# A decoder layer in float32r: the sixteen means of squares as two float32r passes instead of one float32 matmul

## The chip, the core and the metric

The kernel runs on one core of one Trainium2 chip. The metric is device microseconds (us) of one execution; the times below are of three runs. The profile is of one further execution of the same program.

## The reference

One inference step of a one-layer decoder, for a prompt of 256 tokens and a sample batch of 8 x 8 tokens (320 columns together), width 2048:

```
z = rmsnorm(x, g_mix) @ w_in                      # 2048 -> 3584
b, c, hc, q, k, v, qx = split(z)                  # conv gates, 8 q heads, 2 kv heads, 4 cross heads
q, k, qx = rmsnorm(q), rmsnorm(k), rmsnorm(qx)    # per head of 128
y_conv = b * short_conv(c * hc)
y_swa  = sink_attention(q, k, v, window 128, relative bias)
y_x    = cross_attention(qx, memory keys, memory values)
x = x + concat(y_conv, y_swa, y_x) @ w_out
x = x + square(relu(rmsnorm(x, g_mlp) @ w_up)) @ w_down
rmsnorm(x, g) = x * rsqrt(mean(x * x) + 1e-6) * g
```

## The kernel before

**Layout and the large products.** Activations lie transposed: features on the 128 partitions, the 320 tokens along the free axis. A weight piece (128 x 2 x 512) is loaded into `raw` (four buffers), split by ScalarE into its rounded part `wh` (float32r) and by VectorE into the rest `wl`, and each product is three float32r matmuls of 128x320, `wh` by S0h, `wh` by S0l, `wl` by S0h (lines 462 to 464), where S0h and S0l (later S1h and S1l) are the activations split in the same way. These are the rows `mm<-S0h,wh` and so on. A group is one block of 512 output columns: 192 such matmuls into four PSUM banks `mm`. The groups go in the order: cross q, k and v, memory k, memory v (these two with 512 columns), q0, q1, C, H, B, four groups of w_out, then w_up and w_down in four rounds. There are four `mm` banks, so the first matmul into a bank of the next group waits until the bank was read out ("evacuated").

**The side jobs.** All small work (norms, attention, bias) is written as Python generators, the jobs (`Side`, line 206). After each unit of 12 matmuls `boundary()` runs evacuations that are due, and then lets each active job issue its next piece (`side.step()`). A job asks for a buffer (`need`) or waits in a Python model of the engines' clocks (`Pace`, line 93; `after`, line 272) before it issues. So numbers in `Pace.cost` and the count of `yield`s set where a job's instructions stand in each engine's queue. On the chip each engine then takes its queue in that order, and waits at the head of it until the operand is there.

**The means.** A mean of squares over the 128 partitions is one float32 matmul with a matrix of constants, so that the mean stands on every partition: `ones_d` (1/2048) in `mean_rsqrt` (line 517; used for `rb`, the input norm's factor, and once for the MLP norm), `ones_h` (1/128) in `start_head` (line 580; once for each of 4 cross heads, 2 k heads and 8 q heads). Sixteen in all. `newton_terms` (line 353) follows on ScalarE: Ln, Exp, Square.

**Two places where the program holds the matmuls back.** The evacuations of the first group multiply by `rb`, so the second group's first matmul cannot be issued before rb's job has finished (`if waiting: side.until(["rb"])`). And the evacuation of the first bank of group C needs a buffer that the prompt's cross attention gives back:

```
def c_evac(m, ps):
    if m == 0:
        side.until(["convpre"])
```

`side.until` issues side jobs step by step, and no large matmul, until the named job is done. "convpre" (line 1035) waits for "cp", `cross_prompt_all` (line 770), which works off the four cross heads one after another: scores into a bank, maximum, exponential, reciprocal, scaling, four transposes, copy, product with the values.

`z` tiles come from ten slots (`zs`, line 269); a head holds z and y and later a.

Of the kernel before, what the change touches and what calls it, by code (L numbers as in the profile page):

```python
# [9 lines left out]
F32 = mybir.dt.float32  # L10
F32R = mybir.dt.float32r
AF = mybir.ActivationFunctionType
ALU = mybir.AluOpType
AX = mybir.AxisListType

P = 128
# [6 lines left out]
T = TP + TS  # L23
# [224 lines left out]
def trunk_step(ctx: ExitStack, tc: tile.TileContext, I, O):  # L248
# [4 lines left out]
    pe, act, dve = (Paced(pace, n, e) for n, e in (("pe", nc.tensor), ("act", nc.scalar), ("dve", nc.vector)))  # L253
    pool, sp = Paced(pace, "pool", nc.gpsimd), Paced(pace, "dma", nc.sync)

    const = ctx.enter_context(tc.tile_pool(name="const", bufs=1))
# [12 lines left out]
    zs = Slots(zp, "z", 10)  # L269
    lx = Slots(lxp, "lx", 4)  # L270

    def after(*tiles):
        while not pace.ready(tiles):
            yield 1

    def bank():
        return ax.need([P, 512])

    def zt(cols=336):
        return zs.need([P, 336])  # L280

    def sm(n=8):
        return smp.tile([P, 8], F32, name="sm", tag="sm")
# [21 lines left out]
    ones_h = const.tile([P, P], F32, name="ones_h")  # L305
    dve.memset(ones_h, 1.0 / 128)
    ones_d = const.tile([P, P], F32, name="ones_d")
    dve.memset(ones_d, 1.0 / D)
    eps = const.tile([P, 1], F32, name="eps")
    dve.memset(eps, EPS)  # L310
    col["n_q"], col["n_k"], col["n_x"] = 63, 64, 65
# [29 lines left out]
    def small_rsqrt(out, ss, n, width):  # L341
        v, y, t = sm()[:, 0:n], sm()[:, 0:n], sm()[:, 0:n]
        dve.tensor_scalar(out=v, in0=ss, scalar1=1.0 / width, scalar2=EPS, op0=ALU.mult, op1=ALU.add)
        yield from after(v)
        act.activation(out=y, in_=v, func=AF.Ln)
        act.activation(out=y, in_=y, func=AF.Exp, scale=-0.5)
        act.activation(out=t, in_=y, func=AF.Square)
        yield from after(t)
        dve.tensor_tensor(out=t, in0=v, in1=t, op=ALU.mult)
        dve.tensor_scalar(out=t, in0=t, scalar1=-0.5, scalar2=1.5, op0=ALU.mult, op1=ALU.add)  # L350
        dve.tensor_tensor(out=out, in0=y, in1=t, op=ALU.mult)

    def newton_terms(y, a, mean):
        act.activation(out=y, in_=mean, func=AF.Ln, bias=eps)
        act.activation(out=y, in_=y, func=AF.Exp, scale=-0.5)
        act.activation(out=a, in_=y, func=AF.Square)
        yield from after(a)
        dve.scalar_tensor_tensor(out=a, in0=mean, scalar=EPS, in1=a, op0=ALU.add, op1=ALU.mult)
# [158 lines left out]
    def mean_rsqrt(out, sq):  # L517

        yield from after(sq)
        bk = yield from bank()  # L520
        pe.matmul(out=bk[:, 0:T], lhsT=ones_d, rhs=sq, start=True, stop=True)
        yield 1
        y = yield from zt()
        yield from newton_terms(y[:, 0:T], out, bk[:, 0:T])
        ax.put(bk)
        dve.tensor_scalar(out=y[:, 0:T], in0=y[:, 0:T], scalar1=-0.5, scalar2=None, op0=ALU.mult)
        dve.scalar_tensor_tensor(out=out, in0=out, scalar=-3.0, in1=y[:, 0:T], op0=ALU.add, op1=ALU.mult)
        zs.put(y)

    def rb_job():  # L530
        for b in range(4):
            act.activation(out=xblk[b], in_=xblk[b], func=AF.Square)
            if b % 2:
                yield 1
                dve.tensor_tensor(out=xblk[b - 1], in0=xblk[b - 1], in1=xblk[b], op=ALU.add)
        yield 1
        s = xblk[0]
        dve.tensor_tensor(out=s, in0=s, in1=xblk[2], op=ALU.add)
        lx.put(xblk[1], xblk[2], xblk[3])
        dve.tensor_tensor(out=s[:, 0:2, :], in0=s[:, 0:2, :], in1=s[:, 2:4, :], op=ALU.add)  # L540
        dve.tensor_tensor(out=s[:, 0, :], in0=s[:, 0, :], in1=s[:, 1, :], op=ALU.add)
        yield from mean_rsqrt(rb, s[:, 0, :])
        lx.put(s)

    def mem_job():
# [27 lines left out]
        ax.put(bk)  # L573
        w2.put(sq)
        yield from small_rsqrt(rm, tot, 2, D)


    turn = [0]

    def start_head(name, ps, gain, dest):  # L580
        z = zs.must([P, 336])
        dve.tensor_tensor(out=z[:, 0:T], in0=ps, in1=rb, op=ALU.mult)

        def gen():
            while side.now < turn[0]:
                yield 1
            turn[0] = side.now + 2
            y = yield from zt()
            yield from after(z)
            act.activation(out=y[:, 0:T], in_=z[:, 0:T], func=AF.Square)  # L590
            yield 1
            yield from after(y)
            bk = yield from bank()
            pe.matmul(out=bk[:, 0:T], lhsT=ones_h, rhs=y[:, 0:T], start=True, stop=True)
            yield 1
            a = yield from zt()
            yield from newton_terms(y[:, 0:T], a[:, 0:T], bk[:, 0:T])
            ax.put(bk)
            dve.scalar_tensor_tensor(out=z[:, 0:T], in0=z[:, 0:T], scalar=gain, in1=y[:, 0:T],
                                     op0=ALU.mult, op1=ALU.mult)  # L600
            zs.put(y)
            dest(lambda out, v: dve.scalar_tensor_tensor(out=out, in0=v(a), scalar=-3.0, in1=v(z),
                                                         op0=ALU.add, op1=ALU.mult))
            zs.put(a, z)

        side.add(name, gen())
# [73 lines left out]
    def mk_job():  # L680
        ss, r = sm(), sm()
        zz = [st.pop("mkz0"), st.pop("mkz1")]
        junk = yield from half()
        for t in range(2):
            for h in range(XH):
                act.activation(out=junk[:, 0:P], in_=zz[t][:, h * P:(h + 1) * P], func=AF.Square,
                               accum_out=ss[:, t * 4 + h:t * 4 + h + 1])
        w2.put(junk)
        yield from after(ss)
        yield from small_rsqrt(r, ss, 8, 128)  # L690
        st["mkT"] = yield from lx.need([P, XH, MEM])
        for t in range(2):
            for h in range(XH):
                s = zz[t][:, h * P:(h + 1) * P]
                dve.scalar_tensor_tensor(out=s, in0=s, scalar=r[:, t * 4 + h:t * 4 + h + 1], in1=gkx,
                                         op0=ALU.mult, op1=ALU.mult)
            pool.dma_start(out=O["p_mk"][0, 0, t * P:(t + 1) * P].rearrange("k h d -> k (h d)"), in_=zz[t])
        for t in range(2):
            yield from after(zz[t])
            bk = yield from bank()  # L700
            for h in range(XH):
                pe.transpose(bk[:, h * P:(h + 1) * P], zz[t][:, h * P:(h + 1) * P], ident)
            yield 1
            act.activation(out=st["mkT"][:, :, t * P:(t + 1) * P], in_=bk.rearrange("p (h k) -> p h k", h=XH),
                           func=AF.Copy)
            ax.put(bk)
            w2.put(zz[t])
# [408 lines left out]
    def out_evac(g):  # L1116
        def f(m, ps):
            k = g * 4 + m
            a = acc[g][:, m, :]
            dve.tensor_tensor(out=a, in0=ps, in1=a, op=ALU.add)  # L1120
            act.activation(out=S0h[:, k, :], in_=a, func=AF.Copy, scale=gcol("g_mlp", k))
            z = st["sqa"] if k == 0 else zs.must([P, 336])
            act.activation(out=z[:, 0:T], in_=a, func=AF.Square)

            def rest():
                dve.scalar_tensor_tensor(out=S0l[:, k, :], in0=a, scalar=gcol("g_mlp", k),
                                         in1=S0h[:, k, :].bitcast(F32), op0=ALU.mult, op1=ALU.subtract)
                if k:
                    dve.tensor_tensor(out=st["sqa"], in0=st["sqa"], in1=z[:, 0:T], op=ALU.add)
                    zs.put(z)  # L1130
                if k == 15:
                    side.add("r2", mean_rsqrt(st["r2b"], st["sqa"]))

            later.append(rest)
        return f
# [65 lines left out]
    bk = ax.must([P, 512])  # L1201
# [74 lines left out]
```

## Time and profile before

| what | value |
|---|---|
| median of three runs | 1342.4 us (1342.21 to 1344.62) |
| the profiled execution's own time | 1342.93 us |
| its span, first to last instruction | 1341.1 us |
| TensorE (PE) busy | 1322.6 us, 99% |
| VectorE (DVE) busy | 655.8 us, 49% |
| ScalarE (ACT) busy | 533.0 us, 40% |
| mean granted TensorE clock | 0.994 |

PE, DVE, ACT, POOL and SP are the five engines; PEld is the weight load, which overlaps PE. Every instruction that passes through the recording helper carries its line, L166, so groups are told apart by their tiles: `mm<-S0h,wh` is a matmul that writes an mm bank. A float32 matmul that isn't a transpose appears as two rows of the trace, a float32r matmul and a transpose as one. A row of the timeline is: start, duration, engine, line, operation, tiles, shape, count, and in brackets the idle time of the engine before it with what ended it. The clock column gives the share of the full TensorE clock that was granted.

### The profile page before, as it was taken

The numbers are of one execution on the slowest core, as the hardware profiler recorded it, in microseconds if no ns is written. First come the engines' busy times: TensorE is split into PE (matmuls) and PEld (weight loads), VectorE is DVE, ScalarE is ACT, GpSimd is POOL, SyncE is SP. The second block draws the span as 40 slices with busy tenths as digits, with TensorE's granted clock in tenths as the row PEclk, the third lists the DMA queues.
The fourth block names the chain that finished last, engine by engine and source line by source line (L and its number), as shares of the span: only waits on it lengthen the run. The fifth ranks groups of instructions, "written<-read, shape, count | busy, mean of one in ns | idle before, by whom it ended". The sixth has DMA issues, their size and how long they took to land.

```text
span 1341.1 us, 21456 instructions
## 1 busy us (share of the span) xinstructions
PE 1322.6 (99%) x8938; PEld 1294.7 (97%) x8938; DVE 655.8 (49%) x974; ACT 533.0 (40%) x771; POOL 15.6 (1%) x32
## 2 busy tenths in 40 slices
PE   8799999999999999999999999999999999999998
PEld 8787999989999999999999999999999999999998
DVE  6575456785455544444344443434444434444342
ACT  7555355433344444323334432233443233444221
POOL 0010000000000000000000000000000000000000
PEclk9899999999999999999999999999999999999999
DMA  8567653436644445444454444444444444445452
GB/s 301 185 203 252 213 182 132 145 111 224 211 157 142 142 148 167 143 157 138 146 161 154 145 139 157 156 152 149 142 141 160 156 156 143 141 150 166 163 175 71
DMA packets 64880, 217.03 MB, mean 162 GB/s; under 512 B 8357, under 2 KB 10125, under 8 KB 64752
## 3 DMA queue, kind: packets, MB, share of 16 engines
q1 hardware_dynamic: 62752, 210.38, 47.4%
q0 software_dynamic: 1744, 5.19, 1.1%
q8 instruction: 70, 1.15, 0.4%
q14 instruction: 26, 0.21, 0.0%
q10 hardware_dynamic: 288, 0.10, 0.0%
HBM read 211.53 MB, written 7.65 MB: 163 GB/s over the span
## 4 chain that ended last, share of the span: by engine, by line
PE 95%; DVE 2%; ACT 1%; DMA 1%; issue 0%; SPq 0%; DVEq 0%; ACTq 0%
PE mm L166 91%; PE ax L166 4%; DVE z L166 1%; DVE wl L166 1%; ACT wh L166 0%; DMA w<-in_cmk 0%; DVE lx L166 0%; DMA raw<-in_w_in 0%; DVE sm L166 0%; ACT lx L166 0%; ACT w L166 0%; DVE w L166 0%; DVE S1l L166 0%; ACT z L166 0%; SPq L166 0%
## 5 line engine op out<-in xcount | busy, mean ns | idle before, releaser
L166 DVE TENSOR_TENSOR wl<-raw,wh 128x1024 fp32r<-128x1024 f32 (+1 forms) x361 | 437.4, 1220 | 557.8 <-ACT wh L166 554.5
L166 ACT ACTIVATE wh<-raw 128x1024 fp32r<-128x1024 f32 (+1 forms) x361 | 375.1, 1053 | 661.7 <-PE mm L166 613.5
L166 PE MATMUL mm<-S0h,wh 128*128 128x320 f32 x1472 | 463.0, 315 | 12.6 <-DVE z L166 9.7
L166 PE MATMUL mm<-S0h,wl 128*128 128x320 f32 x1472 | 456.6, 310 | 0.2 <-DVE wl L166 0.2
L166 PE MATMUL mm<-S0l,wh 128*128 128x320 f32 x1472 | 456.4, 310 | 0.0
L166 PE MATMUL mm<-S1h,wl 128*128 128x320 f32 x1280 | 395.5, 309 | 0.0
L166 PE MATMUL mm<-S1l,wh 128*128 128x320 f32 x1280 | 395.5, 309 | 0.0
L166 PE MATMUL mm<-S1h,wh 128*128 128x320 f32 x1280 | 395.5, 309 | 0.0
L166 PEld LDWEIGHTS mm<-S0h,wh 128*128 128x128 f32 x1472 | 277.9, 189 | 16.5 <-ACT S1h L166 8.2
L166 PEld LDWEIGHTS mm<-S0l,wh 128*128 128x128 f32 x1472 | 278.0, 189 | 0.8
L166 PEld LDWEIGHTS mm<-S0h,wl 128*128 128x128 f32 x1472 | 277.9, 189 | 0.4 <-DVE wl L166 0.4
L166 PEld LDWEIGHTS mm<-S1h,wh 128*128 128x128 f32 x1280 | 240.2, 188 | 0.0
L166 PEld LDWEIGHTS mm<-S1l,wh 128*128 128x128 f32 x1280 | 240.2, 188 | 0.0
L166 PEld LDWEIGHTS mm<-S1h,wl 128*128 128x128 f32 x1280 | 240.2, 188 | 0.0
L166 ACT ACTIVATE z<-z 128x320 f32<-128x320 f32 x108 | 50.0, 468 | 68.6 <-DVE z L166 67.7
L166 DVE TENSOR_TENSOR S1l<-z,S1h 128x320 fp32r<-128x320 f32 x68 | 33.3, 490 | 51.6 <-ACT S1h L166 51.6
L166 DVE TENSOR_TENSOR acc<-mm,acc 128x320 f32<-128x320 f32 x60 | 29.2, 487 | 34.8 <-PE mm L166 34.8
L166 ACT ACTIVATE S1h<-z 128x320 fp32r<-128x320 f32 x68 | 32.1, 472 | 8.7 <-DVE z L166 6.7
L166 DVE SCALAR_TENSOR_TENSOR z<-mm,r2b 128x320 f32<-128x320 f32 x64 | 30.9, 483 | 0.0
L166 PE MATMUL mm<-wh,S1h 128*128 128x512 f32 x64 | 26.2, 410 | 0.0
L166 PE MATMUL mm<-wl,S1h 128*128 128x512 f32 x64 | 25.0, 391 | 0.0
L166 PE MATMUL mm<-wh,S1l 128*128 128x512 f32 x64 | 25.0, 391 | 0.0
(148 smaller groups left out, 418.4 us busy)
## 6 DMA issues: line engine op xcount, KB each, us to landing
raw<-in_w_up SPq DMA_DIRECT2D x128, 512.0 KB, 3.3
raw<-in_w_down SPq DMA_DIRECT2D x128, 512.0 KB, 3.3
raw<-in_w_in SPq DMA_DIRECT2D x56, 512.0 KB, 3.6
raw<-in_w_out SPq DMA_DIRECT2D x32, 512.0 KB, 3.4
raw<-in_w_mem_k SPq DMA_DIRECT2D x8, 512.0 KB, 3.9
w<-in_cmk SPq DMA_DIRECT2D x16, 256.0 KB, 5.6
raw<-in_w_mem_v SPq DMA_DIRECT2D x8, 512.0 KB, 4.1
w<-in_cmv SPq DMA_DIRECT2D x16, 256.0 KB, 4.6
```

The source lines that it names most:

```text
L166: return f(*args, **kw)
```

## The change

Two constant matrices in float32r are added, and a helper that splits the squares into the rounded part (ScalarE copy to float32r) and the rest (VectorE subtraction), and adds up two float32r matmuls into the same bank. Both users of a mean call it.

```
+    mean_h = const.tile([P, P], F32R, name="mean_h")
+    dve.tensor_copy(out=mean_h, in_=ones_h)
+    mean_d = const.tile([P, P], F32R, name="mean_d")
+    dve.tensor_copy(out=mean_d, in_=ones_d)
...
+    def mean_over(bk, y, scale):
+
+        hi = yield from zs.need([P, 336], F32R)
+        lo = yield from zs.need([P, 336], F32R)
+        act.activation(out=hi[:, 0:T], in_=y, func=AF.Copy)
+        dve.tensor_tensor(out=lo[:, 0:T], in0=y, in1=hi[:, 0:T].bitcast(F32), op=ALU.subtract)
+        yield 1
+        yield from after(lo)
+        pe.matmul(out=bk[:, 0:T], lhsT=scale, rhs=hi[:, 0:T], start=True, stop=False)
+        pe.matmul(out=bk[:, 0:T], lhsT=scale, rhs=lo[:, 0:T], start=False, stop=True)
+        yield 1
+        zs.put(hi, lo)
...
-        pe.matmul(out=bk[:, 0:T], lhsT=ones_d, rhs=sq, start=True, stop=True)
-        yield 1
+        yield from mean_over(bk, sq, mean_d)
...
-            pe.matmul(out=bk[:, 0:T], lhsT=ones_h, rhs=y[:, 0:T], start=True, stop=True)
-            yield 1
+            yield from mean_over(bk, y[:, 0:T], mean_h)
```

A head now passes through one more step, and holds two more of the ten z slots meanwhile. The side jobs therefore come to stand elsewhere in the queues, up to the last head. Two places matter below.

The first is ScalarE's queue around `rb`, while the first group of matmuls ends. `w_2`, `w_3`, `w_5` are blocks of the memory input that the job "mem" splits (S1h) and squares; `z<-ax,eps`, `z<-z`, `rb<-z` are the Ln, Exp and Square of rb's job. Before:

```order
L166 ACTIVATE S1h<-w_2_318,cols 128x256
L166 ACTIVATE z_495<-ax_469,eps 128x320
L166 ACTIVATE z_495<-z_495 128x320
L166 ACTIVATE rb<-z_495 128x320
L166 ACTIVATE w_2_318<-w_2_318 128x512
L166 ACTIVATE S1h<-w_3_320,cols 128x256 x2
L166 ACTIVATE w_3_320<-w_3_320 128x512
```

And now, beginning with the new copy of the sum of squares (z_474 is `hi`):

```order
L166 ACTIVATE z_474<-lx_128 128x320
L166 ACTIVATE wh<-raw 128x1024
L166 ACTIVATE w_6_496<-ax_461 8x384
L166 ACTIVATE S1h<-w_2_322,cols 128x256
L166 ACTIVATE w_2_322<-w_2_322 128x512
L166 ACTIVATE S1h<-w_3_324,cols 128x256 x2
L166 ACTIVATE w_3_324<-w_3_324 128x512
L166 ACTIVATE z_516<-ax_473,eps 128x320
L166 ACTIVATE z_516<-z_516 128x320
L166 ACTIVATE rb<-z_516 128x320
L166 ACTIVATE S1h<-w_5_469,cols 128x256 x2
L166 ACTIVATE w_5_469<-w_5_469 128x512
```

The three steps of rb's job now stand behind the squares of `w_2` and `w_3`. On VectorE the last steps of rb's job have likewise moved behind the two S1l pieces and the sum of the block `w_5`.

The second place is PE's queue in group C, between the 168th and the 169th of its 192 matmuls, where `c_evac` calls `side.until`. `ident` rows are transposes, `vnat` and `vns` are values of the window attention, `kT` and `qT` its keys and queries, `lx` on the right is the values of the cross attention. Before, all that stands there:

```order
L166 MATMUL ax_2504<-ident,w_65_2398 128x128 x4
L166 MATMUL ax_2515<-ident,w_66_2406 128x128 x2
L166 MATMUL ax_2521<-w_71_2513,vnat 128x256 x2
L166 MATMUL ax_2526<-w_72_2524,vnat 128x256
L166 MATMUL ax_2528<-ident,z_2414 128x128
L166 MATMUL ax_2528<-ident,z_2414 64x128
L166 MATMUL ax_2538<-kT,qT 128x256 x2
L166 MATMUL ax_2541<-z_2533,vns 128x128
L166 MATMUL ax_2541<-z_2533,w_64_2278 128x32 x4
L166 MATMUL ax_2560<-w_69_2500,qs 32x128 x4
L166 MATMUL ax_2560<-kT,qs 128x64
```

And now the middle twelve rows of eighteen (two rows of transposes stand ahead of them, and four rows behind, which continue the same jobs):

```order
L166 MATMUL ax_2498<-w_61_2496,vnat 128x256
L166 MATMUL ax_2511<-kT,qT 128x256 x2
L166 MATMUL ax_2528<-ident,w_60_2481 128x128 x4
L166 MATMUL ax_2539<-w_66_2537,lx_1404 128x256 x2
L166 MATMUL ax_2542<-ident,w_65_2514 128x128 x4
L166 MATMUL ax_2547<-kT,qT 128x128 x2
L166 MATMUL ax_2561<-w_63_2504,qs 32x128 x4
L166 MATMUL ax_2561<-kT,qs 128x64
L166 MATMUL ax_2567<-w_67_2551,vnat 128x256 x2
L166 MATMUL ax_2599<-ident,w_68_2553 128x128 x2
L166 MATMUL ax_2609<-ident,z_2573 128x128
L166 MATMUL ax_2609<-ident,z_2573 64x128
```

The fourth cross head (`w_60`, `w_66`) ended 36 matmuls ahead of this place before; now its scores are multiplied 12 matmuls ahead of it, right behind the mean of the last q head, and the rest of it stands inside. `w_65` is made from the scores in ax_2511, `w_68` from those in ax_2547 and `z_2573` from ax_2561: scores, and the transposes of what becomes of them, now stand in one run without a large matmul between.

## The prediction, put down before the changed kernel was timed

> **What bounds the kernel now.** I read the page first, then PE's waits, then the chain of waits. The page's head and its clock row:
>
> ```profile
> span 1341.1 us, 21456 instructions
> ...
> PE 1322.6 (99%) x8938; PEld 1294.7 (97%) x8938; DVE 655.8 (49%) x974; ACT 533.0 (40%) x771; POOL 15.6 (1%) x32
> ...
> PEclk9899999999999999999999999999999999999999
> ```
>
> PE is the bound all along, so what the change takes from PE counts in full, and every wait of PE counts in full as well. PE's waits name their causes (total, times, longest):
>
> ```profile
> PE mm L166 <- DVE z L166: 9.7, 2, 7.9
> ...
> PE ax L166 <- DMA w<-in_cmk: 0.6, 1, 0.6
> ```
>
> The 7.9 us is the wait for `rb`. The other wait for DVE z, 9.7 - 7.9 = 1.8 us, stands at the change from group H to B. So there is little slack to gain, and what matters is what a mean costs on PE, and whether a wait grows. The chain of waits (start, length, piece) prices a mean:
>
> ```profile
> 47.57 13.19 PE mm L166 x72
> 60.76 1.61 PE ax L166 x6
> 62.37 3.52 PE mm L166 x24
> 65.89 0.54 PE ax L166 x2
> ```
>
> A float32 mean is two rows of the trace: 1.61/3 = 0.54 us each time. A float32r matmul of the same shape takes 3.52/24 = 0.147 us.
>
> **The change, part by part.**
>
> *The passes.* Two float32r passes take 2 x 0.147 = 0.294 us, 0.246 less than before. The mean of rb stands ahead of PE's long wait and gains nothing; the other 15 stand in a dense stream: 15 x 0.246 = **-3.7 us**.
>
> *The split.* It adds 16 ScalarE copies and 16 VectorE subtractions. Their nearest rows have the same shape and types:
>
> ```profile
> L166 DVE TENSOR_TENSOR S1l<-z,S1h 128x320 fp32r<-128x320 f32 x68 | 33.3, 490 | 51.6 <-ACT S1h L166 51.6
> ...
> L166 ACT ACTIVATE S1h<-z 128x320 fp32r<-128x320 f32 x68 | 32.1, 472 | 8.7 <-DVE z L166 6.7
> ```
>
> That is 16 x 0.49 = 7.8 us on an engine that is 49% busy and 7.6 us on one that is 40% busy. Where PE has other matmuls in its queue, this costs nothing: the stream of large matmuls covers it. Without that cover, one head's chain would be about 1 us longer. The two added casts of constants run while DVE waits for the first weights. For the MLP norm (one mean, after w_out) the next reader is the evacuation of a whole group of 192 matmuls, 192 x 0.147 = 28 us, so it is covered.
>
> *rb, where the cover is gone.* PE has nothing else in its queue while it waits for rb. The timeline, ScalarE, then VectorE, then PE:
>
> ```profile
> 40.82 0.50 ACT L166 ACTIVATE z<-ax,eps 128x320 f32<-128x320 f32 x1
> ...
> 42.23 0.61 ACT L166 ACTIVATE w<-w 128x512 f32<-128x512 f32 x1
> ...
> 44.39 0.63 ACT L166 ACTIVATE w<-w 128x512 f32<-128x512 f32 x1 [0.75 <-DVE S1l L166]
> 44.92 1.04 ACT L166 ACTIVATE wh<-raw 128x1024 fp32r<-128x1024 f32 x1
> 45.87 0.89 ACT L166 ACTIVATE S1h<-w,cols 128x256 fp32r<-128x256 f32 x2
> ```
> ```profile
> 43.48 0.87 DVE L166 SCALAR_TENSOR_TENSOR S1l<-w,cols,S1h 128x256 fp32r<-128x256 f32 x2
> 45.05 0.69 DVE L166 TENSOR_TENSOR w<-w,w 128x512 f32<-128x512 f32 x1 [0.69 <-ACT w L166]
> 45.66 0.48 DVE L166 SCALAR_TENSOR_TENSOR rb<-ax,rb 128x320 f32<-128x320 f32 x1
> ...
> 46.93 0.49 DVE L166 TENSOR_TENSOR z<-mm,rb 128x320 f32<-128x320 f32 x1
> ```
> ```profile
> 47.57 0.61 PE L166 MATMUL mm<-S0h,wh 128*128 128x320 f32 x1 [7.94 <-DVE z L166]
> ```
>
> The square of `w_2` waited at 42.23 for memory work that does not move, so it and the square of `w_3` (44.39) stay where they are. Ln, Exp and Square, which ran from 40.82 to 42.23 (1.41 us), now start when the square of `w_3` is done, 44.92, and end at 46.33. Then come, ahead of rb's last steps in VectorE's queue: S1h of `w_5` (0.89), the second S1l (half of 0.87, and 0.1 from engine to engine), the square (0.63) and the sum (0.61 to the next start): 46.33 + 0.89 + 0.54 + 0.63 + 0.61 = 49.0. From rb's first VectorE step to PE's restart took 47.57 - 45.66 = 1.91: PE restarts at about 50.9 to 51.1, **+3.5 us**. At least it is the 1 us of the new hop alone; at most 4.5, if the blocks' loads are late too.
>
> *Group C, where a new wait comes.* The cross attention's last head and two pieces of window attention now stand in PE's queue as one run, with scores, and transposes of what VectorE and ScalarE make of these scores, behind each other. PE can't pass them. The same kinds of work before the change (VectorE, ScalarE, PE):
>
> ```profile
> 218.88 0.75 DVE L166 TENSOR_REDUCE sm<-ax 128x1 f32<-128x256 f32 x2
> ```
> ```profile
> 227.77 0.48 DVE L166 SCALAR_TENSOR_TENSOR z<-ax,z 128x320 f32<-128x320 f32 x1
> ...
> 229.22 0.15 DVE L166 RECIPROCAL sm<-sm 128x2 f32<-128x2 f32 x1
> ...
> 235.38 0.42 DVE L166 SCALAR_TENSOR_TENSOR w<-ax,w 128x256 f32<-128x256 f32 x1
> ...
> 237.70 1.22 DVE L166 TENSOR_TENSOR wl<-raw,wh 128x1024 fp32r<-128x1024 f32 x1
> ...
> 244.71 0.67 DVE L166 SCALAR_TENSOR_TENSOR w<-ax,w 128x512 f32<-128x512 f32 x1
> ...
> 246.41 0.55 DVE L166 TENSOR_TENSOR lx<-mm,rb 128x256 f32<-128x256 f32 x2
> ...
> 248.62 0.17 DVE L166 RECIPROCAL sm<-sm 128x2 f32<-128x2 f32 x1
> ...
> 249.36 0.28 DVE L166 TENSOR_TENSOR S1l<-ax,S1h 128x128 fp32r<-128x128 f32 x1
> ```
> ```profile
> 240.86 0.90 ACT L166 ACTIVATE w<-ax 128x512 f32<-128x512 f32 x2 [0.80 <-issue]
> ...
> 246.39 0.51 ACT L166 ACTIVATE w<-w,sm 128x256 f32<-128x256 f32 x1 [0.49 <-DVE sm L166]
> ...
> 247.39 0.19 ACT L166 ACTIVATE sm<-sm 128x2 f32<-128x2 f32 x1
> ```
> ```profile
> 241.51 1.56 PE L166 MATMUL ax<-w,vnat 128*128 128x256 f32 x6 [0.17 <-ACT w L166]
> ```
>
> Prices: two maxima 0.75; a head's last four steps 1.45; bias and maximum of a 512-wide block 1.70; of a 256-wide block with the sample's 2.32; two exponentials 1.0; reciprocal and two scalings 0.74; copies of 512 and 256 columns about 0.55 and 0.35. Transposes are about 0.11 each on PE and a 256-wide product 1.56/3, without its tail 0.43.
>
> Count from the mean of the last q head (0). PE does it, the cross scores (0.9) and 12 large matmuls, and enters the run at about 3.2. Six transposes and a wait for ScalarE's copy of the last two (0.5) bring it with ax_2498 and ax_2511 to 5.7. VectorE meanwhile ends the tails of three heads (the last can't start before the mean, Ln, Exp and Square are through; 4.85), takes the two maxima (5.7 to 5.9), and has in its queue, ahead of the reciprocal, two S1l pieces (0.6) and the 512-wide block (1.70): 8.2. Reciprocal and scaling: 8.95. PE stood from 5.7 to 8.95: 3.2. Four transposes, wait for the copy 0.65, product to 10.9; transposes, scores, sample scores and a product to 13.35. The scores of 11.8 take 2.32 on VectorE plus one S1l, reciprocal and scaling (the exponentials overlap), 1.2: 15.3, so PE stands 2.0. The sample's tail then costs 0.7 and 0.1. Waits in all 0.5 + 3.2 + 0.65 + 2.0 + 0.7 + 0.1 = **+7.2 us**. If VectorE's queue held nothing but the chains, the first wait would vanish and the others total about 4.5; if a key load issued inside the run lands late, 10.
>
> *The granted clock.* Two stretches around rb's wait, then the stretch around group C (columns: stretch, length, PE, PEld, DVE, ACT, POOL busy, granted clock, DMA share, GB/s):
>
> ```profile
> 42.70:52.80 10.10, 5.23 (x20) 5.26 (x21) 6.90 (x14) 4.30 (x9) 2.12 (x3) 0.50 0.68 258
> 52.90:61.00 8.10, 8.10 (x56) 8.02 (x55) 2.96 (x3) 3.08 (x5) 0.00 (x0) 1.00 0.31 113
> 227.00:257.00 30.00, 29.67 (x201) 26.67 (x199) 23.15 (x77) 12.55 (x37) 0.00 (x0) 1.00 0.43 142
> ```
>
> After rb's wait the clock was at half for 5.3 us of matmuls: 13.19 - 72 x 0.147 = 2.6 us lost. That loss stays, since PE restarts later by about as much as the clock is restored later. Around group C PE was busy 29.67 of 30 us at full clock. With waits of 3.2 and 2.0 us there, the clock may be halved once more: 0 to 3.4 us, **+1.5** taken, about half of the one loss seen. The Trainium skill (TensorE: Matmul & The Clock Gate, "What's actually happening") has the clock halved after an idle window of about 3.4 us; no single wait of my walk is that long, and by that rule alone this term would be 0 and the sum 1.5 lower. The 7.94 us wait agrees with the rule but can't show its limit.
>
> *Small ones.* The 0.6 us wait for a memory key load: the loads now stand further ahead of their use, -0.3 (0 to -0.6). Group H to B: VectorE's work between the first and the last evacuation,
>
> ```profile
> 281.92 0.48 DVE L166 TENSOR_TENSOR z<-mm,rb 128x320 f32<-128x320 f32 x1
> ...
> 295.24 0.48 DVE L166 TENSOR_TENSOR z<-mm,rb 128x320 f32<-128x320 f32 x1
> ```
>
> 13.3 us, held PE for 1.8; in the new order one 512-wide block less (-1.4) stands between: -1.0 (0 to -1.8).
>
> *Sum:* -3.7 + 3.5 + 7.2 + 1.5 - 0.3 - 1.0 = **+7.2 us**. On the profiled execution (span 1341.1, its own time 1342.9) that is 1350.1; on the median of the runs, which lies 0.5 lower, **1349.6 us**.
>
> **The rivals.** (a) *The run in group C stays dense*, because its inputs are made in time: -3.7 + 3.5 - 0.3 - 1.0 = -1.5, **1340.9**. For it: before, eleven rows stood there too, and PE waited 0.17 us at them. Against: there no scores stood ahead of their own transposes. (b) *Faster:* as (a), and rb's factor comes at its old time, as it would if the memory blocks' squares were done before rb's sum: -3.7 - 1.3 = **1337.4**. It decides if PE restarts before 47.6 + 1. ScalarE's order speaks against it. (c) *Worse:* the loads of keys and bias that are issued inside the run stand in SP's queue ahead of weight pieces and wait for buffers that the run frees, so PE waits for a load or for weights as well, 4 to 6 us: **1354.6**. Against: weights are four pieces ahead. (d) *The passes don't gain*, a float32r pass with this stationary matrix taking half a float32 one (0.27): +3.7, **1353.3**. Against: 8,000 rows of the same form.
>
> **How the numbers follow.** About 0.2% (2.7 us) is what a measurement of this kernel can tell from no change. Forecast 0.66, (a) 0.12, (b) 0.07, (c) 0.12, (d) 0.03. The forecast's own bounds: -3.7 + 1.0 + 4.5 - 2.4 = -0.6 at the least, with all bounds on one side, -3.7 + 4.5 + 10 + 3.4 = +14.2 at the most; eight in ten over all cases from 1340.5 (which takes in (a)) to 1356. Slower by over 0.2%: the forecast without its lowest tail (0.63), (c), (d): 0.78. Faster: (b) 0.07. Same: the rest, 0.15.
>
> **What would show it.** Rows ax<-z,mean_h of 0.15 us apart, 14 pairs; PE's wait for DVE z at rb about 11.4 in place of 7.9, with PE's restart near 51; and around 238 to 258 us a run of ax rows some 16 us long with waits of PE for DVE w, ACT w and DVE z of together 7, and perhaps a granted clock of 0.5 behind it. I am wrong if PE stays dense there, if its restart lies before 49, or if the time is under 1345.

## The result, and the profile after the change

The changed kernel took 1350.84 us (median of four runs, 1350.68 to 1351.83) and the kernel before 1343.04 (1342.21 to 1344.62) on the same chip: a ratio of 1.0064, with a 95% interval of 1.0051 to 1.0076. The change costs 7.8 us. The forecast was 1349.6 us in a range of 1340.5 to 1356. The profiled execution took 1351.83 us, 8.9 more than the one before the change (1342.93).

The page of the changed kernel, its head, engines and clock row:

```profile
span 1350.0 us, 21475 instructions
...
PE 1324.9 (98%) x8938; PEld 1298.0 (96%) x8938; DVE 664.0 (49%) x992; ACT 539.5 (40%) x787; POOL 15.6 (1%) x32
...
PEclk9899999799999999999999999999999999999999
```

PE is busy 2.3 us longer than before, although 16 means got cheaper; the span grew by 8.9. So PE waits more, and the 7 in the eighth slice (236 to 270 us) says that part of its busy time was spent at a lower clock. PE's waits (total, times, longest):

```profile
PE mm L166 <- DVE z L166: 10.3, 1, 10.3
PE ax L166 <- DVE w L166: 4.6, 2, 3.0
...
PE ax L166 <- DVE z L166: 2.0, 3, 1.0
...
PE ax L166 <- ACT w L166: 0.7, 1, 0.7
```

The waits at rows that write an `ax` bank are new, but for 0.2 us for ACT w that stood there before too. Two waits of before are gone: that for a memory key load (0.6), and the second one of large matmuls for DVE z, between group H and B (1.8).

**At rb.** ScalarE, then VectorE, then PE (start, duration, engine, line, operation):

```profile
44.57 0.63 ACT L166 ACTIVATE w<-w 128x512 f32<-128x512 f32 x1 [0.75 <-DVE S1l L166]
45.11 0.51 ACT L166 ACTIVATE z<-ax,eps 128x320 f32<-128x320 f32 x1
...
46.15 0.47 ACT L166 ACTIVATE rb<-z 128x320 f32<-128x320 f32 x1
...
47.97 0.63 ACT L166 ACTIVATE w<-w 128x512 f32<-128x512 f32 x1 [0.55 <-DVE S1l L166]
```
```profile
48.63 0.69 DVE L166 TENSOR_TENSOR w<-w,w 128x512 f32<-128x512 f32 x1 [0.70 <-ACT w L166]
49.24 0.48 DVE L166 SCALAR_TENSOR_TENSOR rb<-ax,rb 128x320 f32<-128x320 f32 x1
```
```profile
51.06 0.64 PE L166 MATMUL mm<-S0h,wh 128*128 128x320 f32 x1 [10.28 <-DVE z L166]
```

Ln starts right behind the square of `w_3`, and rb's first VectorE step right behind the sum of `w_5`, as the new order has them. PE restarts at 51.06 in place of 47.57. Its wait grew by less than that, from 7.94 to 10.28, because the mean of rb now stands behind the last 12 large matmuls and not ahead of them (39.81 in place of 37.07 us).

**In group C.** PE's rows of the run that now stands between two large matmuls, with its five waits in brackets:

```profile
232.82 0.82 PE L166 MATMUL ax<-ident,w 128*128 128x128 f32 x6
234.62 0.67 PE L166 MATMUL ax<-w,vnat 128*128 128x256 f32 x2 [0.98 <-DVE z L166]
...
239.15 1.16 PE L166 MATMUL ax<-ident,w 128*128 128x128 f32 x4 [2.99 <-DVE w L166]
241.00 2.08 PE L166 MATMUL ax<-w,lx 128*128 128x256 f32 x4 [0.69 <-ACT w L166]
...
248.26 0.43 PE L166 MATMUL ax<-ident,w 128*128 128x128 f32 x2 [1.59 <-DVE w L166]
249.40 0.66 PE L166 MATMUL ax<-ident,z 128*128 128x128 f32 x2 [0.71 <-DVE z L166]
...
254.79 0.83 PE L166 MATMUL mm<-S0h,wh 128*128 128x320 f32 x1
```

The waits add up to 6.96 us, and the run lasts from 232.82 to 254.79. The same stretch cut in pieces of 3.4 us (columns: stretch, length, PE, PEld, DVE, ACT, POOL busy, granted clock, DMA share, GB/s):

```profile
231.70:235.10 3.40, 2.42 (x17) 2.18 (x16) 3.30 (x10) 1.07 (x3) 0.00 (x0) 1.00 0.83 261
235.10:238.50 3.40, 1.05 (x5) 0.57 (x4) 3.26 (x11) 1.41 (x5) 0.00 (x0) 1.00 0.67 213
238.50:241.90 3.40, 2.07 (x6) 1.50 (x7) 1.75 (x8) 1.78 (x6) 0.00 (x0) 0.51 0.13 20
241.90:245.40 3.50, 3.50 (x20) 2.52 (x19) 0.55 (x2) 0.98 (x2) 0.00 (x0) 0.50 0.45 129
245.40:248.80 3.40, 1.70 (x8) 1.08 (x8) 3.12 (x16) 1.84 (x10) 0.00 (x0) 1.00 0.24 81
248.80:252.20 3.40, 2.80 (x9) 1.92 (x10) 1.33 (x5) 0.70 (x2) 0.00 (x0) 0.50 0.23 82
252.20:255.60 3.40, 3.40 (x13) 3.04 (x13) 0.50 (x2) 0.28 (x1) 0.00 (x0) 0.50 0.00 0
255.60:259.00 3.40, 3.40 (x20) 2.75 (x18) 3.23 (x16) 1.19 (x5) 0.00 (x0) 0.50 0.00 0
```

The clock was halved twice, for two pieces and for three. VectorE is busy for 3.26 of the 3.4 us in which PE mostly stands (second row): PE waits for what lies ahead in VectorE's queue.

### The profile page after: what moved, and what is told of

Same layout as the page of the kernel before. It is cut to its first block, busy times and chain, and to the rows that moved or that the text cites. A ratio compares the mean times of both kernels' runs of the same rounds, so it can differ in the third digit from the quotient of the medians.

```text
span 1350.0 us, 21475 instructions
## 1 busy us (share of the span) xinstructions
PE 1324.9 (98%) x8938; PEld 1298.0 (96%) x8938; DVE 664.0 (49%) x992; ACT 539.5 (40%) x787; POOL 15.6 (1%) x32
## 4 chain that ended last, share of the span: by engine, by line
PE 94%; DVE 3%; ACT 2%; issue 1%; DMA 0%; SPq 0%; DVEq 0%; ACTq 0%
PE mm L166 91%; PE ax L166 4%; ACT wh L166 1%; DVE z L166 1%; DVE wl L166 1%; ACT z L166 0%; DVE S1l L166 0%; DVE w L166 0%; DMA raw<-in_w_in 0%; DVE lx L166 0%; ACT lx L166 0%; DVE sm L166 0%; ACT w L166 0%; ACT S1h L166 0%; DVE qT L166 0%
## 5 line engine op out<-in xcount | busy, mean ns | idle before, releaser
L166 PE MATMUL mm<-S0h,wh 128*128 128x320 f32 x1472 | 462.1, 314 | 12.5 <-DVE z L166 10.3
L166 ACT ACTIVATE z<-z 128x320 f32<-128x320 f32 (+1 forms) x122 | 56.1, 467 | 72.0 <-DVE z L166 68.3
```

The lines of the kernel that those rows point to most:

```text
L166: return f(*args, **kw)
```

## The experiments

The theory: a pass costs what its row says, so the passes gain 3.7 us, and the loss comes from where the side jobs now stand, at rb and in group C, with the halved clock as a cost of its own. The rivals: the passes don't gain; the split's work on ScalarE and VectorE is what costs, wherever it stands; the clock is free, since PE waits anyhow. Each kernel was timed in five rounds or more beside the kernel before, whose median in the four sets of runs lay between 1342.3 and 1343.1 us.

**1. The same order, float32 means again.** The split is still made, but one float32 matmul reads the squares themselves:

```
-        pe.matmul(out=bk[:, 0:T], lhsT=scale, rhs=hi[:, 0:T], start=True, stop=False)
-        pe.matmul(out=bk[:, 0:T], lhsT=scale, rhs=lo[:, 0:T], start=False, stop=True)
+        nc.tensor.matmul(out=bk[:, 0:T], lhsT=ones_h if scale is mean_h else ones_d, rhs=y, start=True, stop=True)
...
```

> Every instruction stands where it stands in the changed kernel, the split of the squares too, but each of the 16 means is one float32 matmul again, of the squares themselves (the rounded part and the rest are made and not used). Theory (a pass of float32r costs 0.147 us, a float32 mean 0.54, and PE is the bound): 15 means of the dense stream cost 0.246 us more each and rb's as well, so 1350.8 + 3.9 = 1354.7 us. Rival (the passes gain nothing, all of the change comes from somewhere else): 1350.8 us, within 0.7.

Measured: 1353.96 us, ratio to before 1.0085 [1.0071, 1.0099], so 3.1 us above the changed kernel. Matmuls of a head's mean, in the changed kernel and here (least, median, greatest ns of one of the 28 rows):

```profile
L166 PE MATMUL ax<-z,mean_h x28: 303/308/414, 63.1 to 230.1; 128*128 128x320 f32 x28
```
```profile
L365 PE MATMUL ax<-z,ones_h x28: 430/432/436, 64.1 to 233.7; 128*128 128x320 f32 x28
```

Two rows a mean, 0.124 us apart each: 0.248 a mean, against 0.246 forecast. The rival without a gain falls. The 0.8 that is missing to 3.9 is within the two intervals. The clock differs between the two traces as well: here it was halved for one piece fewer in group C, but behind rb's wait for 5.6 us (50.93 to 56.56) and not for 3.2 (51.06 to 54.22).

**2. rb ahead of the memory blocks.** The memory job pauses from the sum of squares until rb is there:

```
+        side.flags.add("hold")
         yield from mean_rsqrt(rb, s[:, 0, :])
...
         for i in range(8):
+            while "hold" in side.flags and "rb" not in side.flags:
+                yield 1
             t = mblk.pop(i)
```

> The changed kernel, but the job that splits the memory input pauses from the moment the sum of squares for rb is there until rb is there, so Ln, Exp and Square of rb's job stand ahead of the squares of the blocks w_2 and w_3 in ScalarE's queue. Theory (rb is late because of its place in the queues): PE restarts at 47.0 to 48.0 us in place of 51.06 and the time falls by 3.0 to 4.0, to 1347.3 us, with group C as it was (waits of 8 us in its run). Rival (rb is late by the longer chain of the split alone, about 1 us, or by the loads of its input): restart at 50 or later, 1350 us.

Measured: 1347.48 us, 1.0040 [1.0026, 1.0053], 3.4 less than the changed kernel. PE's restart, and two new waits later:

```profile
42.87 0.63 PE L166 MATMUL mm<-S0h,wh 128*128 128x320 f32 x1 [3.60 <-DVE z L166]
...
88.61 0.62 PE L166 MATMUL ax<-w,w 128*32 128x256 f32 x4 [0.43 <-DMA w<-in_cmk]
90.09 0.62 PE L166 MATMUL ax<-w,w 128*32 128x256 f32 x4 [0.85 <-DMA w<-in_cmk]
```

The place in the queue is the cause: the chain with the split needs only 3.6 us of PE's time, not 10.3. The restart came 8.2 us earlier and not 3 to 4 as expected, but only 3.4 of them reached the end by the medians, and 5.7 by the profiled executions (1346.15 against 1351.83, the fastest of five runs and the slowest of four). Between the two traces 1.3 went to the two waits for key loads, which now come late, and about 1.1 to the clock: behind the restart it was at half for 5.5 us (42.87 to 48.35), in the changed kernel for 3.2. Group C kept its run.

**3. No run in group C.** The convolution's buffer is taken from the free fourth slot, so that `c_evac` has nothing to wait for:

```
-    side.add("convpre", conv_pre_job(), needs=["cp"], cost=1)
+    side.add("convpre", conv_pre_job(), needs=["mix"], cost=1)
```

> The changed kernel, but the convolution's buffer is taken from the fourth slot of its pool as soon as the memory values are there, so that the first evacuation of group C has nothing to wait for and no large matmul is held back. Theory (the run of small matmuls in group C costs 7.9 us of waits, and the halved clock around it 4 to 6 more): no wait of PE over 1 us between 225 and 262 us, granted clock 1.0 there, and 12 us less; the tail of the last window attention now comes due inside the first group of w_out and gives 3 to 5 back: 1342.5 us (1340 to 1345). Rival (the waits come from work of VectorE and ScalarE that the split has added, and follow it wherever it stands): 1348 to 1351 us.

Measured: 1353.97 us, 1.0087 [1.0073, 1.0101]: a miss, 11.5 us over the forecast. Around 225 to 262 us the waits and the halved clock are gone. But PE now waits at two other places: a sample's scores stand still for a load of keys, and the last attention's tail has come into the first group of w_out, with four waits of which this is the longest:

```profile
292.56 0.66 PE L166 MATMUL ax<-w,qs 128*32 128x128 f32 x8 [6.07 <-DMA w<-in_csk]
...
342.24 0.72 PE L166 MATMUL ax<-ident,w 128*128 128x128 f32 x4 [2.37 <-DVE w L166]
```

SyncE's queue says why the keys are late (its rows last as long as the issue is held):

```profile
277.53 6.92 SPq L166 DMA_DIRECT2D raw<-in_w_in  x2
284.50 5.20 SPq L166 DMA_DIRECT2D w<-in_csk  x1
```

The key load stood behind two weight pieces that waited 6.9 us for their buffers, and then waited itself. That is a wait of the kind of the prediction's rival (c), with the parts exchanged: there key loads stand ahead of weight pieces, here one stood behind them. The run can be taken away, and its cost with it; what the moved jobs meet instead was as dear.

**4. The waits of the run filled with matmuls.** Constant matmuls into the banks that the transposes overwrite, 40 ahead of the wait of 2.99 us and, not shown here, 20 ahead of the wait of 1.59 us:

```
+    def fill(bk, n):
+        for _ in range(n if st.get("run") else 0):
+            nc.tensor.matmul(out=bk[:, 0:P], lhsT=mean_h, rhs=mean_h, start=True, stop=True)
...
         bk = yield from bank()
+        fill(bk, 40 if h == 3 else 0)
```

> The changed kernel, with 40 matmuls of a constant 128x128 matrix set in PE's queue ahead of the transposes at which PE waits 3.2 us in the run of group C, and 20 ahead of the transposes at which it waits 1.75 us. They are overwritten and leave nothing out; 40 x 0.06 = 2.4 us and 20 x 0.06 = 1.2 us lie inside the waits. Theory (the halved clock is a cost of its own, worth 4 to 6 us): the clock stays at 1.0 from 238 to 245 us and perhaps to 259, the waits still end when they ended, and the time falls to 1346 us (1345 to 1348). Rival (the clock costs nothing, since PE has to wait for VectorE anyhow): 1350 to 1351 us.

Measured: 1347.90 us, 1.0045 [1.0032, 1.0058], 2.9 less than the changed kernel, with more work on PE, and inside the theory's range. The run's PE rows, and the pieces of 3.4 us:

```profile
237.16 4.68 PE L754 MATMUL ax<-mean_h 128*128 128x128 f32 x40 [0.49 <-DVE S1l L166]
241.68 0.62 PE L166 MATMUL ax<-ident,w 128*128 128x128 f32 x4
```
```profile
237.10:240.50 3.40, 3.34 (x30) 3.34 (x30) 2.85 (x11) 2.06 (x9) 0.00 (x0) 1.00 0.22 74
240.50:243.90 3.40, 2.71 (x21) 2.38 (x20) 0.74 (x3) 0.60 (x1) 0.00 (x0) 1.00 0.11 37
```

The clock stayed at 1.00 through the run. A filling matmul took 0.113 us (4.52 / 40), not 0.06, so the forty lasted longer than the wait: counted from the product ahead of them (235.14 here, 234.62 in the changed kernel), the transposes came 2.0 us later. If these 2.0 us reached the end in full, the halved clock cost 2.9 + 2.0, about 5 us. That they did is an estimate: VectorE was busy for only 0.74 us of the second piece, so there it waited for PE and not PE for it. At the least the clock cost the 2.9 us that were seen, and the rival that it costs nothing falls.

**5 and 6. The split beside the square, no further step.** The heads' squares are split in the step that makes them, and the tile of squares is given back:

```
+            hi = yield from zs.need([P, 336], F32R)
+            lo = yield from zs.need([P, 336], F32R)
             act.activation(out=y[:, 0:T], in_=z[:, 0:T], func=AF.Square)
+            act.activation(out=hi[:, 0:T], in_=y[:, 0:T], func=AF.Copy)
+            dve.tensor_tensor(out=lo[:, 0:T], in0=y[:, 0:T], in1=hi[:, 0:T].bitcast(F32), op=ALU.subtract)
+            zs.put(y)
             yield 1
-            yield from after(y)
+            yield from after(lo)
...
```

> The changed kernel, but in the heads the squares are split in the same step in which they are made, so a head takes as many steps as before the change, and its tile of squares is given back at once; rb's mean stays as in the changed kernel. PE's queue then has one product of the window attention between the 168th and 169th matmul of group C in place of the run of some 40 rows. Theory (what costs is the additional step of each head, which brings the run about; the passes themselves gain 0.246 us each): no wait of PE over 1 us between 225 and 262 us, granted clock 1.0 there, rb as late as in the changed kernel (restart 50.5 to 51), and 1350.8 - 12 + 1 = 1340 us (1338 to 1342). Rival (split and passes cost what the changed kernel lost, wherever they stand, or a load of keys comes late as it did with the early buffer): 1346 to 1351 us.

> As the kernel with the split beside the square, and the memory job pauses until rb is there. Theory: the two repairs add up, restart at about 43 us, no run in group C, 1340 - 3.4 = 1336.5 us (1334 to 1339), below the kernel before the change. Rival (what is won at rb is lost again at the loads of the memory keys, or the clock): 1339 to 1342 us.

Measured: 1346.93 us (1.0033 [1.0021, 1.0045]), and with the pause of the memory job as well 1339.91 us (0.9985 [0.9976, 0.9994]). Both missed their ranges and came out in those of the rivals. The run in group C is gone, with no wait over 1 us there, as expected, and rb is as late as in the changed kernel (the same wait of 10.28 us), but only 3.9 us came off; 11 less was forecast. Most of the rest sits in group B; PE's waits in the kernel without the pause:

```profile
PE mm L166 <- DVE z L166: 12.3, 4, 10.3
PE ax L166 <- DVE z L166: 3.2, 2, 3.0
```

Beside the 10.3 us for rb these are three short waits of large matmuls (0.53 at 82.53 us, 0.56 and 0.94 in group B), and one of 3.0 us that ends at 309.84 us at a sample's transposes, around which the clock was halved for 6.8 us. The kernel with the pause has the same waits in group B, the last one shorter (1.76), and waits 0.57 and 0.72 us for loads of memory keys and values. So the theory was too narrow in one point: it is not the run in group C alone. Each of these orders puts some small matmul right behind what it needs.

**7. The pause alone, in the kernel before** (float32 means, the edit of experiment 2):

> The kernel before the change (float32 means), with the pause of the memory job alone. It shows what the pause is worth without the passes. Theory: PE's restart moves from 47.6 to about 42 us; of these 5.5 us some 2 to 3 arrive at the end, as 3.4 of 8.2 did with the changed kernel: 1340 us (1338.5 to 1341.5); the kernel with the split beside the square and the pause is 3.5 us faster than this one, 15 x 0.246 = 3.7. Rival (with the restart so early nothing else in the passes counts): the two are equal within 1 us.

Measured: 1336.16 us, 0.9957 [0.9944, 0.9970]. It is faster than both kernels, and by more than expected: 6.5 us. The restart came at 43.24, only 4.3 us earlier. Its trace shows two more gains: behind the restart the clock was at half for 3.1 us (43.24 to 46.33) and not for 5.3 (47.57 to 52.88), about 1.0 us, and the wait for a memory key load (0.6) is gone. With it, the kernel without the passes is 3.8 us faster than experiment 6 with them; I had forecast 3.5 slower.

**8. Float32 means in the heads only**; rb and the MLP norm keep two passes:

> The changed kernel with one float32 mean in each of the 14 heads, as before the change; the two means of rb and of the MLP norm keep their two passes. Theory (rb's delay is one cost, the heads' order another): restart of PE at 50.7 to 51.1 us, no run of 16 us in group C, 1342.5 + 3.5 = 1346.0 us (1345 to 1347.5). Rival (the later rb moves the side jobs on, so the run in group C comes without the heads' additional step as well): 1354 us.

Measured: 1346.67 us, 1.0030 [1.0018, 1.0042]. The time is right, the reason half: PE restarts at 51.19, but this order too has a wait in group C,

```profile
229.60 0.69 PE L166 MATMUL ax<-ident,w 128*128 128x128 f32 x2 [3.71 <-DVE w L166]
```

with 6.8 us at half clock from 228.40 us on. So the step in rb's mean alone moves the side jobs of group C. What made up for this wait I can name only in part: the waits for a memory key load (0.6) and between H and B (1.8) are gone, and behind rb's restart the clock was at half for 3.1 us (51.19 to 54.32) and not for 5.3.

**9 and 10. The passes alone, in an unchanged order.** Each head's mean is two passes over the rounded squares (ScalarE's square written as float32r), with constants of half the size; the rest of the squares is left out. The model of the engines' clocks is told of one float32 matmul, so that nothing moves:

```
-            pe.matmul(out=bk[:, 0:T], lhsT=ones_h, rhs=y[:, 0:T], start=True, stop=True)
+            for first in (True, False):
+                nc.tensor.matmul(out=bk[:, 0:T], lhsT=mean_h, rhs=y[:, 0:T], start=first, stop=not first)
+            pace.issue("pe", "matmul", bk[:, 0:T], [ones_h, y[:, 0:T]])
...
```

> The kernel before the change with every instruction in its old place, but each of the 14 heads' means is two float32r passes over the rounded squares, with constants half as large; the rest of the squares is left out, so there is no split and no further step. Theory (the passes gain what a row says, and the order alone cost what the changed kernel lost): 14 x 0.246 = 3.4 us less than before, 1342.7 - 3.4 = 1339.3 us (1338.2 to 1340.5). Rival (what PE wins at a mean it waits for at the next evacuation or load): 1342 to 1343 us.

> The same passes, the rest left out again, in the order of the kernel before with the paused memory job (1336.2 us). Theory: 1336.2 - 3.4 = 1332.8 us (1331.8 to 1334). Rival, as for the order of before: 1335.5 to 1336.5 us.

Measured: 1339.03 us (0.9975 [0.9966, 0.9984]; 3.5 less than the 1342.56 of before), and 1333.33 us in the order with the pause (0.9933 [0.9920, 0.9945]; 2.8 less than experiment 7). Both as the theory has it. What a pass saves arrives at the end, in the order of before in full, when nothing moves.

**11 and 12. The whole split, in an unchanged order.** Copy and subtraction right behind the square, unseen by the model of the clocks (as in experiment 12; in 11 `hi` is one tile `hi_b` for all heads):

```
             act.activation(out=y[:, 0:T], in_=z[:, 0:T], func=AF.Square)
+            hi, lo = w2.must([P, 512], F32R), zs.must([P, 336], F32R)
+            nc.scalar.activation(out=hi[:, 0:T], in_=y[:, 0:T], func=AF.Copy)
+            nc.vector.tensor_tensor(out=lo[:, 0:T], in0=y[:, 0:T], in1=hi[:, 0:T].bitcast(F32), op=ALU.subtract)
             yield 1
             yield from after(y)
...
```

> The whole computation: the heads' squares are split into the rounded part and the rest right behind the square (14 copies on ScalarE, 14 subtractions on VectorE), and two passes add them up, while everything else stands in the order of the kernel before with the paused memory job. The rounded part has one tile of its own, one more z slot is held for the rest, and the side jobs' clock does not see the split. Theory (split hidden, order kept): as without the split, 1332.8 us (1331.8 to 1334.2), the fastest of all. Rival (the chain of a head, 1 us longer by copy and subtraction, makes PE wait at the means): 14 means at up to 0.5 us, 1336 to 1340 us.

> The whole computation again: the heads' squares split right behind the square, two passes, everything else in the order of the kernel before with the paused memory job, and the rounded part in a buffer that each head takes from the attention's pool of twelve, so no head writes over another's. Theory (split hidden, passes gain 14 x 0.246, order kept): as fast as the two passes without the split in this order, 1333.3 us (1332.3 to 1334.8), 9 us less than the kernel before and 17 less than the changed one. Rival (the head's chain is 1 us longer, and PE waits at the means): 1335.5 to 1340 us, with waits of PE for DVE z or ACT w at the rows of the means.

Measured: 1336.98 us (0.9960 [0.9948, 0.9973]) and 1336.36 us (0.9953 [0.9940, 0.9967]). In experiment 11 the heads share one tile `hi_b`, and twice, at a k head (copies at 78.06 and 79.42 us, the first one's mean at 80.14) and at a q head (167.38, 169.67 and 170.20), the next head's copy comes ahead of a mean, which then reads the rounded squares of the wrong head: its results are wrong. Its time agrees with that of experiment 12, which has no such overlap. Neither reached 1333. The fourth cross head's mean in experiment 12, PE and VectorE:

```profile
61.53 0.31 PE L602 MATMUL ax<-w,mean_h 128*128 128x320 f32 x1
63.47 0.41 PE L603 MATMUL ax<-z,mean_h 128*128 128x320 f32 x1 [1.62 <-DVE z L598]
```
```profile
59.26 1.23 DVE L166 TENSOR_TENSOR wl<-raw,wh 128x1024 fp32r<-128x1024 f32 x1 [0.24 <-ACT wh L166]
...
62.92 0.48 DVE L598 TENSOR_TENSOR z<-z,w 128x320 fp32r<-128x320 f32 x1
```

The subtraction stood behind a weight piece's split and seven smaller VectorE pieces, and PE waited 1.62 us for it. So the split is not free where no step is left for it. That explains about half of the 3 us between experiments 10 and 12; the profiled run of 12 also had a half clock from 290.6 to 294.0 us, and started its first matmul 1.0 us later. How much of the medians' difference these two make is open; experiment 11 has the same wait of 1.62 us without a halved clock there. So the rival that the split costs something wherever it stands holds in part: with the heads' whole split in the order of experiment 7 the time is 1336.4 us, against 1336.2 without split and passes. Within what these runs can tell, the split took back there what the passes had won.

## Why the prediction was right, and where it was not

*The passes*, -3.7: shown. 0.248 us a mean by the rows, 3.5 us for 14 heads by experiment 9 (2.8 in the order of experiment 10). Rival (d) falls.

*The split*, hidden: VectorE's busy time grew by 8.2 us (7.8 forecast), ScalarE's by 6.5 (7.6), and PE waited for it twice, 0.50 and 0.35 us. The helper gives it a step of its own, and that step is what moves everything else. In experiments 5 and 6 it has none, but the job still waits for it in the model of the clocks, and PE waits at no head's mean. Experiment 12 shows the other side: where nothing waits for it, the order is kept and PE meets the subtraction.

*rb*, +3.5: the restart came at 51.06, the walk had 50.9 to 51.1. Its queue, square by square, was the one in the rows: Ln at 45.11 (44.92 in the walk), rb's first VectorE step at 49.24 (49.0). Experiment 2 shows the cause by removing it. Rival (b) falls. One step failed beside it: "That loss stays", of the halved clock behind rb. PE restarted 3.5 us later, but the clock came back only 1.3 us later (54.22 against 52.88), so that 3.2 us of matmuls and not 5.3 ran at half, and about 1.0 us of the 3.5 came back at once. In the fourteen traces this stretch lasted from 3.1 to 6.1 us, so that a single trace could not have told its length.

*Group C*, +7.2: the waits 0.98, 2.99, 0.69, 1.59 and 0.71 stand for the walk's 0.5, 3.2, 0.65, 2.0 and 0.7; their sum, 6.96, is right within 0.3. By the profile the first of them was for VectorE (DVE z), where the walk had ScalarE's copy, and it was twice as long as in the walk. Only the run's length was off, 22.0 us and not 16, which is the clock's part. Rival (a) falls.

*The granted clock*, +1.5 with bounds 0 and 3.4: this is the term that was mis-sized, and it came out beyond its bounds as far as experiment 4 can tell. I took "about half of the one loss seen" at rb. The step that failed is "halved once more": the clock was halved twice, for 17 us together, once around the wait of 2.99 us and once behind that of 1.59 us. Experiment 4 puts the cost at 4.9 us by the medians and at 5.9 by the profiled executions (3.9 + 2.0), with its 2.0 us of overrun counted in full; 2.9 of it were seen.

*The small ones*, -0.3 and -1.0: the key load's wait and that between H and B went entirely, -0.6 and -1.8, each at the bound given.

The terms with their measured sizes: -3.7 + 3.5 - 1.0 (the clock behind rb) + 7.0 + 4.9 - 0.6 - 1.8 = +8.3, or +9.3 with 5.9 for the clock in group C, against 8.9 between the two profiled executions. The clock's 3.4 us too little were made up in part by 1.0 us behind rb, 1.1 in the small terms and 0.2 in the waits. That the forecast's +7.2 lies so close to the medians' 7.8 is therefore partly luck.

Rival (c), late loads behind others in SyncE's queue, did not happen in the changed kernel, where PE waited for no load. A wait of its kind, of 6.07 us, came in experiment 3.

What experiments 3, 5 and 8 add is that I could price one given order from its rows, and could not say what the next order would bring: the forecasts for these three kernels, whose order I had not walked through, were off by up to 11.5 us, or right for half the reason.

## What to carry to other kernels

Where a program's own planner sets the order of small work, a cheaper instruction that needs one more step is first of all a new order: price the saving by its row, then walk the new queues at each place where the large work is held back, because there a few microseconds of VectorE work come to stand in front of TensorE. Test the two apart, by the old instruction in the new order and the new instruction in the old order; here these were +3.1 and -3.5 us, while the change as a whole cost 7.8. With the pause of experiment 7 and the order kept, the whole split came out as fast as the float32 means: what the saving needs beside itself belongs in its price. And where a new wait may also halve the clock, put that down as a cost of its own: here 7.0 us of waits brought about an estimated 5 us more.

## What the runs showed of the hardware

The granted clock changes only on a grid. In every trace the changes lie whole multiples of 3.41 us apart (in the changed kernel 54.2, 238.5, 245.4, 248.8 and 259.0 us: 54, 2, 1 and 3 steps), and where the grid lies differs from run to run. So the same wait may cost half a clock or nothing: the wait at the change from group H to B is 1.74 or 1.75 us long in six traces, and the clock was halved behind it in that of experiment 12 alone. In experiments 7 and 12 it falls as follows (the columns are those of the stretches above):

```profile
285.30:288.70 3.40, 1.98 (x13) 1.72 (x12) 3.29 (x7) 0.00 (x0) 0.00 (x0) 1.00 0.00 0
288.70:292.10 3.40, 3.07 (x21) 3.07 (x22) 3.26 (x16) 1.99 (x2) 0.00 (x1) 1.00 0.46 159
```
```profile
287.20:290.60 3.40, 1.66 (x12) 1.40 (x11) 3.29 (x7) 0.00 (x0) 0.00 (x0) 1.00 0.07 11
290.60:294.00 3.40, 3.40 (x14) 3.40 (x14) 3.33 (x14) 2.11 (x2) 1.03 (x2) 0.50 0.39 148
```

With 1.98 us of PE work in the step the clock stayed, with 1.66 it was halved for the next. In the changed kernel steps with 1.05 and 1.70 us were followed by half clock, and one with 2.42 was not. Busy time alone doesn't decide, though: in experiment 5 a step with 2.47 us (304.35 to 307.76) was followed by half clock, and in experiment 1 a step with 1.53 us by full clock,

```profile
237.50:240.90 3.40, 1.53 (x6) 1.06 (x6) 3.33 (x11) 1.67 (x7) 0.00 (x0) 1.00 0.97 321
240.90:244.30 3.40, 0.94 (x5) 0.58 (x6) 2.78 (x11) 1.85 (x7) 0.00 (x0) 1.00 0.01 5
244.30:247.70 3.40, 3.40 (x12) 2.78 (x12) 0.00 (x0) 0.98 (x2) 0.00 (x0) 0.50 0.40 88
```

and in the changed kernel the step from 252.2 to 255.6, with PE busy throughout but mostly with narrow matmuls, was followed by another at half clock. What exactly is counted stays open. The Trainium skill (TensorE: Matmul & The Clock Gate, "What's actually happening") has such a window, 3413 ns long and free-running, and the grid agrees with it. The Trainium skill's advice on the same page ("Why this matters for your kernels"), to avoid idle gaps over about 3 us, is not enough by these rows: a wait of 1.59 or 1.74 us within one step sufficed.

And a float32r matmul of 128 columns took 0.113 us in experiment 4, against 0.147 for 320 columns: the narrow one has 40% of the columns and costs about three quarters as much.
